# Long convolutions with the inverse second stage in float32r parts and a first stage that stacks both parts of two residues on its rows

## The chip, the core and the metric

The kernel runs on one core of a Trainium2 chip. The metric is the device time of one execution in microseconds. The engines are TensorE (PE in the profile; PEld are its weight loads), VectorE (DVE), ScalarE (ACT), GpSimd (POOL) and SyncE (SP), which here only starts transfers. Each engine works through its own instructions in order; semaphores make it wait for another engine or for a DMA.

## What is computed

One layer of a bidirectional encoder: a normalisation, one input projection, two head groups (four mLSTM heads and a Hyena operator of order two), an output projection and a squared-ReLU MLP. The change lies in the Hyena part, whose two long convolutions over 2048 positions and 512 channels are written in the reference as an FFT of length 4096:

```python
def two_sided_fft_conv(u, k_fwd, k_bwd, bias):
    kern = jnp.concatenate([k_fwd, jnp.zeros_like(k_fwd[:1]), k_bwd[:0:-1]], axis=0)
    K = jnp.fft.rfft(kern, axis=0)
    U = jnp.fft.rfft(u, n=2 * S, axis=1)
    y = jnp.fft.irfft(U * K[None], n=2 * S, axis=1)[:, :S]
    return y + u * bias
...
z = cv[..., OFF_HV:OFF_HV + H_WIDTH]
z = cv[..., OFF_HX1:OFF_HX1 + H_WIDTH] * two_sided_fft_conv(z, filt[:, 0, 0], filt[:, 1, 0], fb[0])
z = cv[..., OFF_HX2:OFF_HX2 + H_WIDTH] * two_sided_fft_conv(z, filt[:, 0, 1], filt[:, 1, 1], fb[1])
```

## The kernel before

The transform of 4096 points is done as two stages of 64 (4096 = 64 x 64), each a product with a constant matrix on TensorE over tiles of 128 rows by 512 channels. The first stage works on the positions that share a residue modulo 64: 16 tiles h in a convolution, four residues in each tile of input. Its result goes to DRAM (`d1`), sorted by the 32 frequencies j of the first stage. The second stage takes one j at a time, here called a turn: it transforms the kernel's tile (`dk`, made earlier by `filter_spectra`) and the data's tile (`d1`) with the same matrix `c_s2[j]`, multiplies the two spectra, and transforms back with `c_s2i[j]`; that result goes to DRAM (`d2`). Between the two convolutions the inverse first stage is done (`py`), the gate is multiplied in, and the first stage of convolution 1 follows at once (`first`, with o = 1). The inverse first stage of convolution 1 comes much later and is not touched.

Most products are float32 products made of three float32r ones. `split` writes a rounded upper part on one engine (`hi`, ACT) and the rest on another (`low`, POOL or DVE), and `mm3` adds up w_low x_hi, w_hi x_low and w_hi x_hi (lines 159 to 161). The inverse second stage is the exception: it multiplies whole float32 operands (line 1187), which the chip runs as two instructions.

In a turn of the second stage (lines 1175 to 1204, all from `hyena`) the names are: `prepare(j)` splits the matrix and the two tiles of residue j; `pk` is the kernel's spectrum (made by `spectrum`, copied to SBUF by `kept`); `pu` is the data's spectrum; `product(j)` multiplies them on DVE into `z`; `pi` is the inverse product for the turn before last, copied to `st` by ACT and stored. Loads are started three turns ahead (`kernel_loads`, `data_loads`), with the inverse matrix `ci` in its own turn. Tiles come from rings by tag: 6 tiles `raw`, 4 `hi`, 4 `z`, 4 `c`, 2 `cr`, 3 `ci`. A load into a ring waits until the tile's last reader is done, and SP holds all later loads behind it.

The order is that of the program text, for each engine alone. The long convolutions run as a generator, and each `yield` names how much of the input projection (`work`: matrix products, their evictions and stores) is put in before the generator goes on (`drive`). So the projection's products stand between those of the convolution on TensorE, and its casts, scalings and loads between the others on their engines.

Of the kernel before, what the change touches and what calls it, by code (L numbers as in the profile page):

```python
# [8 lines left out]
F32 = mybir.dt.float32  # L9
# [18 lines left out]
SPLIT = {"w4", "s1k"}  # L28
# [16 lines left out]
def host_constants():  # L45
# [15 lines left out]
    s1 = np.zeros((128, 2, 128))  # L61
    s1i = np.zeros((128, 2, 128))
# [4 lines left out]
    for b in range(4):  # L67
        q, r = slice(b, 128, 4), slice(b * 32, b * 32 + 32)
        s1[q, 0, q] = re
        s1[q, 1, q] = im  # L70
        s1i[r, 0, q] = wre.T / 4096
        s1i[r, 1, q] = wim.T / 4096
# [33 lines left out]
    data_row = (p % 2) * 64 + 4 * ((p % 32) // 2) + p // 32  # L106
# [8 lines left out]
    out["c_s1"] = pack(s1, "s1")  # L115
    out["c_s1i"] = pack(s1i, "s1i")
    out["c_s1k"] = pack(s1k, "s1k")
    out["c_s2"] = np.ascontiguousarray(s2[:, data_row, :], dtype=f32)
    out["c_s2i"] = np.ascontiguousarray(s2i[:, :, back_col], dtype=f32)
# [23 lines left out]
    out["c_t"] = np.ascontiguousarray(-np.stack([tn[64 * pa + 8 * (g // 4) + g % 4 + 4 * pb] for g in range(32)], axis=1))  # L143
# [4 lines left out]
class Builder:  # L148
# [258 lines left out]
    def filter_spectra(self, kp, wk, ps, ps2):  # L407
# [20 lines left out]
        def filt(i):  # L428
            g, o = divmod(i, 2)
            lg = lt[g % NB]  # L430
            if o == 0:
                for e in range(2):
                    rows = slice(64 * e, 64 * e + 64)
                    b = 8 * (g // 4) + g % 4
                    src = hv[rows, b:b + 5:4, :]
# [21 lines left out]
        def spread(i, x):  # L457
# [7 lines left out]
            if o == 1:  # L465
                self.load(self.dk.rearrange("j (b h q) o c -> b h j q o c", b=4, h=8)[g % 4][g // 4], st)
# [586 lines left out]
    def hyena(self, pools):  # L1053
# [6 lines left out]
        def raw(src):  # L1060
            t = wk.tile([128, 512], F32R, tag="raw", name="raw", bufs=6)
# [10 lines left out]
        def cols():  # L1072
            return wk.tile([128, 256], F32R, tag="c", name="c", bufs=4)

# [17 lines left out]
        def short(dtype=F32):  # L1092
            return wk.tile([128, 512], dtype, tag="z", name="z", bufs=4)

        def first(o, h, s1, x):

            st, dst = pair(), d1[o].rearrange("j (b h r) c -> h j b r c", b=4, h=16)[h]
            pts = []
            for r in range(2):
                pts.append(bank("p1"))  # L1100
                self.mm3(pts[r], s1[r], x, True, True)
# [3 lines left out]
            self.store(dst, st)  # L1105


        s1 = constant("c_s1")
        x = [raw(self.tile_rows(0, h)) for h in range(4)]
        self.load(self.s1i, io["c_s1i"])  # L1110
        yield 8.0
        s1, y = s1(), {0: parts(x[0])}
        yield 2.0
        for h in range(16):
            if h + 1 < 16:
                y[h + 1] = parts(x[h + 1])
            if h + 4 < 16:
                x.append(raw(self.tile_rows(0, h + 4)))
# [3 lines left out]
        for o in range(2):  # L1122
            kd, rd, c2, ci, kk, zz, pu = ({} for _ in range(7))

            def kernel_loads(j):
                c2[j] = wk.tile([128, 128], F32, tag="cr", name="cr", bufs=2)
                self.load(c2[j], io["c_s2"][j])
# [853 lines left out]
```

## Time and profile before

| | |
|---|---|
| median of 3 runs | 2696.65 us (2690.52 to 2699.77) |
| profiled execution | 2695.04 us |
| its span, first to last instruction | 2693.1 us |
| mean granted TensorE clock | 0.986 |
| PE busy | 2590.1 us, 96% of the span |
| DVE, ACT, POOL busy | 1544.1, 1232.0, 1204.1 us |
| moved by DMA | 465.74 MB, mean 173 GB/s |

Rows of the profile read "line engine operation out<-in shape xcount". Names are the program's with buffer numbers left out, and a line may be that of a helper: line 166 is ACT's cast in `split`, 169 its subtraction, 159 to 161 are the products of `mm3`, 231 and 234 start loads and stores. Rows of the timeline begin with the start in us from the first instruction and the duration in us; what stands in brackets at the end is the idle time before, and what ended it. PE's durations overlap from one product to the next.

The long convolutions lie between about 392 and 1013 us, beside the input projection. Convolution 0 has its first stage until about 465 and its turns from 482; the part between the convolutions runs from about 698 to 797, the turns of convolution 1 from 812.

### The profile page before, as it was taken

Reading aid. Unit: us, or ns where it says so; the run is one execution under the profiler, and the core shown is the slowest. Engines: PE = TensorE matmul, PEld = TensorE weight load, DVE = VectorE, ACT = ScalarE, POOL = GpSimd, SP = SyncE. Lnnn points to the kernel's source line nnn. Section 1 sums busy time; section 2 is a strip of 40 time slices with the busy share of each in tenths; the row PEclk is TensorE's granted clock in tenths of the full one; section 3 lists DMA queues with packets and bytes.
Section 4 is the critical chain, followed back from the end, with each engine's and each line's share of the span. In section 5 each row is a group of like instructions: output and inputs, shape, how many; then the busy total and the mean of one; then the engine's idle time right before and its main releaser. Section 6 shows DMA issues by size and latency. Waiting matters only on the chain.

```text
span 2693.1 us, 35367 instructions
## 1 busy us (share of the span) xinstructions
PE 2590.1 (96%) x12237; PEld 2110.8 (78%) x12237; DVE 1544.1 (57%) x2454; ACT 1232.0 (46%) x2276; POOL 1204.1 (45%) x964
## 2 busy tenths in 40 slices
PE   6999999999999998889997999999999999999998
PEld 5778888777798887767774788868888888888876
DVE  5676653777547665666556444474444443543477
ACT  6355544655544346653334444454444323222344
POOL 1211114555225543446666877677772440301232
PEclk8999999999999999999998999999999999999999
DMA  6233346665676558556765444554447453445555
GB/s 175 61 87 113 114 125 219 194 190 176 217 233 178 185 167 275 180 166 218 241 200 186 156 137 164 184 191 172 146 155 287 147 176 100 130 141 163 181 170 213
DMA packets 288355, 465.74 MB, mean 173 GB/s; under 512 B 37543, under 2 KB 149415, under 8 KB 287153
## 3 DMA queue, kind: packets, MB, share of 16 engines
q1 hardware_dynamic: 227600, 324.85, 38.8%
q10 hardware_dynamic: 53264, 117.53, 11.6%
q0 software_dynamic: 7312, 21.11, 3.1%
q8 instruction: 97, 1.59, 0.2%
q14 instruction: 82, 0.66, 0.1%
HBM read 289.27 MB, written 174.13 MB: 172 GB/s over the span
## 4 chain that ended last, share of the span: by engine, by line
PE 40%; DVE 4%; POOL 4%; DMA 3%; issue 2%; ACT 2%; ACTq 0%; SPq 0%; DVEq 0%; POOLq 0%
PE pm L159 13%; PE pm L160 13%; PE pm L161 13%; DVE cb L169 1%; POOL xt L1265 1%; DMA m<-in_w_mlp_out_dram 1%; DMA hm<-ht 1%; DMA m<-in_w_mlp_in_dram 1%; POOL cb L169 1%; ACT xo L1405 1%; DVE hm L1906 0%; ACTq L234 0%; DVE xo L1408 0%; DVE gss L1307 0%; DVE hm L169 0%
## 5 line engine op out<-in xcount | busy, mean ns | idle before, releaser
L166 ACT CAST cb<-m 128x1024 fp32r<-128x1024 f32 (+1 forms) x342 | 277.9, 849 | 438.0 <-PE pm L159 375.3
L169 DVE TENSOR_TENSOR cb<-m,cb 128x1024 fp32r<-128x1024 f32 (+1 forms) x222 | 237.8, 1109 | 301.0 <-ACT cb L166 300.7
L160 PE MATMUL pm<-cb 128*128 128x512 f32 x880 | 343.6, 390 | 7.8 <-DVE cb L169 7.8
L159 PE MATMUL pm<-hm,cb 128*128 128x512 f32 x840 | 330.8, 394 | 13.9 <-POOL cb L169 8.0
L159 PE MATMUL pm<-cb 128*128 128x512 f32 x880 | 342.4, 389 | 1.2 <-DVE cb L169 1.0
L161 PE MATMUL pm<-cb 128*128 128x512 f32 x880 | 342.6, 389 | 0.0
L160 PE MATMUL pm<-hm,cb 128*128 128x512 f32 x840 | 329.9, 393 | 2.6 <-POOL hm L169 2.5
L161 PE MATMUL pm<-hm,cb 128*128 128x512 f32 x840 | 328.9, 392 | 0.0
L169 POOL TENSOR_TENSOR cb<-m,cb 128x1024 fp32r<-128x1024 f32 x120 | 262.0, 2194 | 61.7 <-ACT cb L166 61.6
L1717 DVE TENSOR_TENSOR m<-pm,m 128x512 f32<-128x512 f32 x224 | 153.9, 690 | 235.0 <-PE pm L161 214.3
L159 PE MATMUL pt<-hn,w 128*128 128x512 f32 x640 | 267.7, 419 | 1.0 <-ACT hn L489 0.9
L169 POOL TENSOR_TENSOR raw<-raw,hi 128x512 fp32r<-128x512 f32 x160 | 206.4, 1302 | 103.0 <-ACT hi L166 76.7
L160 PE MATMUL pt<-hn,w 128*128 128x512 f32 x640 | 252.0, 394 | 0.3 <-DVE hn L490 0.2
L161 PE MATMUL pt<-hn,w 128*128 128x512 f32 x640 | 251.9, 394 | 0.0
L160 PEld LDWEIGHTS pm<-cb 128*128 128x128 f32 x880 | 165.2, 188 | 45.7 <-DVE cb L169 11.7
L159 PEld LDWEIGHTS pm<-hm,cb 128*128 128x128 f32 x840 | 159.0, 189 | 50.0 <-POOL cb L169 10.2
L159 PEld LDWEIGHTS pm<-cb 128*128 128x128 f32 x880 | 165.2, 188 | 36.4 <-ACT junk L1891 1.4
L161 PEld LDWEIGHTS pm<-cb 128*128 128x128 f32 x880 | 165.3, 188 | 33.8
L160 PEld LDWEIGHTS pm<-hm,cb 128*128 128x128 f32 x840 | 159.4, 190 | 36.6 <-POOL hm L169 2.9
L1721 ACT ACTIVATE m<-m 128x512 f32<-128x512 f32 x128 | 80.6, 630 | 233.9 <-DVE m L1717 232.3
L161 PEld LDWEIGHTS pm<-hm,cb 128*128 128x128 f32 x840 | 159.4, 190 | 33.6
L647 POOL DMA_DIRECT2D vp<-vst x96 | 61.3, 643 | 228.1 <-ACT vst L643 227.0
(323 smaller groups left out, 5732.5 us busy)
## 6 DMA issues: line engine op xcount, KB each, us to landing
ga<-m ACTq DMA_DIRECT2D x96, 512.0 KB, 3.4
m<-ga SPq DMA_DIRECT2D x96, 512.0 KB, 4.1
d<-st ACTq DMA_DIRECT2D x64, 512.0 KB, 2.6
m<-in_w_mlp_in_dram SPq DMA_DIRECT2D x64, 512.0 KB, 4.0
m<-in_w_mlp_out_dram SPq DMA_DIRECT2D x114, 256.0 KB, 3.6
raw<-d SPq DMA_DIRECT2D x96, 256.0 KB, 3.0
xt<-in_x_dram SPq DMA_DIRECT2D x32, 512.0 KB, 5.5
dk<-kst SPq DMA_DIRECT2D x32, 512.0 KB, 3.3
```

Source lines behind the costliest of these rows:

```text
L159: pe.matmul(ps, w[1], x[0], start=first, stop=False)
L160: pe.matmul(ps, w[0], x[1], start=False, stop=False)
L161: pe.matmul(ps, w[0], x[0], start=False, stop=last)
L166: self.act.copy(hi, src)
L169: (eng_lo or self.dve).tensor_tensor(lo, src, hi.bitcast(F32), ALU.subtract)
L647: pool.dma_start(dst[:, 8 * b + e:8 * b + 8:2, cc:cc + 128], st[64 * e:64 * e + 64])
L1265: eng.tensor_tensor(res[:, cs], tmp[e], res[:, cs], ALU.add)
L1405: act.activation(x1, xt, AF.Square, accum_out=ss1[:, h:h + 1])
L1717: dve.tensor_tensor(dst, a, b, ALU.add)
L1721: act.activation(g, g, AF.Relu)
```

## The change

Two things change in what is computed, and several in what carries it.

First, the inverse second stage uses `mm3`. Its matrix comes from the host in two parts (256 columns, upper part and rest), as does now `c_s2`; ACT rounds both with one copy (`rounded`), and the subtraction for `c_s2` on POOL is gone. The data `z` is split on the device: a cast on ACT and a subtraction on POOL, one turn after `product` made it.

Second, the first stage no longer takes 128 rows of upper parts and then 128 rows of rests. A tile has 64 positions of two residues; for each half of the tile, `stacked` makes one operand whose one half of the rows holds the upper part of a residue pair and whose other half holds its rest. One product with the upper part of the matrix on both halves, and one with the rest of the matrix on one half and zeros on the other, give what three products gave. The residues are grouped otherwise for this (two neighbouring ones, so `vp` is loaded straight and `d1` is stored in two pieces), and with them the rows of `c_s2` and the filter table. The split of z between the convolutions is made by DVE in halves.

Third, the rings: `raw` has 5 tiles instead of 6, `z` 5 instead of 4, `ci` is gone, and both matrices share the 2 tiles `cr`, now 256 columns wide. With these, `prepare(j + 1)` has moved behind the copy of spectrum j, the data is loaded two turns ahead and the matrix `c_s2` two turns ahead, after the kernel tile.

```diff
+        def stacked(src, tag, eng):
+            ts = [wk.tile([128, 512], F32R, tag=tag, name="hl", bufs=4 if tag == "hi" else 5) for _ in range(2)]
+            for t, p in zip(ts, (slice(0, 64), slice(64, 128))):
+                act.copy(t[p], src[p])
+            for t, p, q in zip(ts, (slice(0, 64), slice(64, 128)), (slice(64, 128), slice(0, 64))):
+                eng.tensor_tensor(t[q], src[p], t[p].bitcast(F32), ALU.subtract)
+            return ts
...
-            for r in range(2):
-                pts.append(bank("p1"))
-                self.mm3(pts[r], s1[r], x, True, True)
+            for g in range(2):
+                pts.append(bank("p1"))
+                pe.matmul(pts[g], s1[0], x[g], start=True, stop=False)
+                pe.matmul(pts[g], s1[1 + g], x[g], start=False, stop=True)
                 yield
...
             for j in range(34):
-                if j + 1 < 32:
-                    prepare(j + 1)
                 if j < 32:
                     pk = spectrum(j)
                     yield 1.3
                     kept(j, pk)
+                    if j + 1 < 32:
+                        prepare(j + 1)
+                    if j + 2 < 32:
+                        data_loads(j + 2)
...
-                    pe.matmul(pi, ci.pop(j - 2), zz.pop(j - 2), start=True, stop=True)
+                    self.mm3(pi, ci.pop(j - 2), zz.pop(j - 2), True, True)
...
+                if 1 <= j < 33:
+                    ci[j - 1] = rounded(ci[j - 1])
+                    zz[j - 1] = parts(zz[j - 1], short(F32R))
                 if j + 3 < 32:
                     kernel_loads(j + 3)
-                    data_loads(j + 3)
-                if j < 31 or j == 31:
-                    ci[j] = wk.tile([128, 128], F32, tag="ci", name="ci", bufs=3)
-                    self.load(ci[j], io["c_s2i"][j])
+                if j + 2 < 32:
+                    c2[j + 2] = matrix(io["c_s2"][j + 2])
+                if j < 32:
+                    ci[j] = matrix(io["c_s2i"][j])
```

How the instructions move on three engines, in a turn of convolution 0. What stands in brackets are the engines and queues that a row waits for. On TensorE (`pt` are the projection's products), before:

```order
L159 MATMUL pk_5014<-hi_4947,c_4944 128x512 [waits Activation_49,Pool_49]
L160 MATMUL pk_5014<-raw_4860,c_4944 128x512 [waits Pool_49]
L161 MATMUL pk_5014<-hi_4947,c_4944 128x512
...
L1187 MATMUL pi_5029<-z_4938,ci_4928 128x512 [waits DMAHW0_49,DVE_49,Activation_49]
L159 MATMUL pt_5031<-hn10_82,w1_92 128x512
```

and in the changed kernel:

```order
L163 MATMUL pk_5108<-hi_5059,c_5057 128x512 [waits Activation_49]
L164 MATMUL pk_5108<-raw_4949,c_5057 128x512 [waits Pool_49]
L165 MATMUL pk_5108<-hi_5059,c_5057 128x512
...
L163 MATMUL pi_5133<-hi_5080,c_5077 128x512 [waits Activation_49]
L164 MATMUL pi_5133<-z_5079,c_5077 128x512 [waits Pool_49]
L165 MATMUL pi_5133<-hi_5080,c_5077 128x512
```

The inverse product waited for DVE and for its matrix; it is now three products, of which the first waits for ACT and the second for POOL.

On SP's queue, where the loads of the second stage stand, before (`raw` from `dk` and `d10` are the kernel's and the data's tile, `qk0` is a store of the projection):

```order
L231 DMA cr_4548<-in_c_s2_dram 128x128 [waits DMAHW4_49,Pool_49]
L231 DMA raw_4550<-dk_65 128x512 [waits DMAHW5_49,PE_49]
L231 DMA raw_4552<-d10_3501 128x512 [waits DMAHW6_49,PE_49]
L231 DMA ci_4554<-in_c_s2i_dram 128x128 [waits DMAHW7_49,DMAHW0_49]
L231 DMA qk0_69<-yc_93 128x512 [waits DMAHW0_49,DVE_49]
```

and in the changed kernel:

```order
L235 DMA raw_4507<-d10_3501 128x512 [waits DMAHW5_49,PE_49]
L235 DMA raw_4541<-dk_65 128x512 [waits PE_49,Pool_49]
L235 DMA cr_4543<-in_c_s2_dram 128x256 [waits DMAHW3_49,Activation_49]
L235 DMA cr_4545<-in_c_s2i_dram 128x256 [waits DMAHW4_49,DMAHW1_49,Activation_49]
L235 DMA qk0_69<-yc_93 128x512 [waits DMAHW2_49,DVE_49]
```

The matrix `c_s2` stood ahead of the two tiles of its residue and now stands behind the kernel tile of the residue after it; both matrices now wait for ACT.

On ACT, before, from one copy of a spectrum (`z<-pk`) on:

```order
L1147 COPY z_5026<-pk_5014 128x512 [waits PE_49]
L607 ACTIVATE yc_93<-pt_4957,cw_64 128x512 [waits DMAHW1_49,PE_49]
L1193 COPY st_5028<-pi_5029 128x512 [waits DMAHW2_49,PE_49]
L166 CAST c_5065<-cr_4978 128x128 [waits DMAHW2_49]
L166 CAST hi_5068<-raw_4980 128x512 [waits DMAHW3_49,Pool_49]
L166 CAST hi_5071<-raw_4982 128x512 [waits DMAHW4_49,PE_49,Pool_49]
```

and in the changed kernel:

```order
L1173 COPY z_4842<-pk_4830 128x512 [waits PE_49]
L1086 CAST c_4844<-cr_4820 128x256 [waits DMAHW7_49]
L170 CAST hi_4846<-raw_4740 128x512 [waits DMAHW6_49]
L170 CAST hi_4849<-raw_4789 128x512 [waits DMAHW4_49,Pool_49]
L610 ACTIVATE yc_93<-pt_4764,cw_64 128x512 [waits DMAHW1_49,PE_49]
L1222 COPY st_4854<-pi_4855 128x512 [waits DMAHW3_49,PE_49]
L1086 CAST c_4875<-cr_4822 128x256 [waits DMAHW0_49]
L170 CAST hi_4878<-z_4824 128x512 [waits DVE_49,Pool_49]
```

The three casts of `prepare` stood behind the copy of `pi` and now stand ahead of it, behind the copy of the spectrum; the rounding of the inverse matrix and the cast of z are new behind it.

## What I predict, and from what

> **What bounds the kernel now.** I read the page first (TensorE is busy for 96% of the span), then cut the busy times at the borders of the long convolutions, then asked what TensorE itself waits for there. Columns of the first view: stretch, its length, busy time and instructions of PE, PEld, DVE, ACT and POOL, granted clock, DMA share, GB/s.
>
> ```profile
> 392.00:469.00 77.00, 77.00 (x355) 62.91 (x355) 28.78 (x53) 31.36 (x56) 36.46 (x39) 1.00 0.66 221
> 469.00:690.00 221.00, 221.00 (x911) 170.50 (x910) 164.35 (x271) 122.68 (x231) 113.20 (x113) 1.00 0.62 188
> 690.00:800.00 110.00, 107.46 (x619) 94.10 (x618) 56.92 (x110) 52.25 (x96) 31.68 (x26) 0.98 0.70 228
> 800.00:1013.00 213.00, 210.00 (x1400) 185.03 (x1398) 140.84 (x245) 98.92 (x197) 106.53 (x110) 0.99 0.58 176
> ```
>
> These are the first stage of convolution 0, its 32 turns, the part between the convolutions, and the 32 turns of convolution 1. TensorE is idle for 5.5 of 621 us. The waits of TensorE in the same time (engine line <- releaser: sum, times, longest) are as few:
>
> ```profile
> PE pt L159 <- ACT w L166: 2.1, 1, 2.1
> PE py L159 <- ACT hi L166: 1.3, 1, 1.3
> PE py L160 <- POOL raw L169: 0.8, 1, 0.8
> ```
>
> So this stretch lasts as long as its products, and those of the projection are poured in between by fixed weights that the change leaves alone. A product removed here is worth its full time, and any new wait of TensorE costs its full time: the rest of the program follows behind.
>
> **What the change removes.** The timeline of TensorE around one inverse product (start, duration, engine, operation):
>
> ```profile
> 565.55 0.40 PE L161 MATMUL pt<-hn,w 128*128 128x512 f32 x1
> 565.78 1.02 PE L1187 MATMUL pi<-z,ci 128*128 128x512 f32 x2
> 566.24 0.80 PE L159 MATMUL pt<-hn,w 128*128 128x512 f32 x1
> 566.88 0.40 PE L160 MATMUL pt<-hn,w 128*128 128x512 f32 x1
> ```
>
> Durations overlap, so the price is the distance of starts: 0.23 us from one float32r product to the next. From 565.55 to 566.88 are 1.33 us; less two plain products (0.46) the float32 inverse takes 0.87 us. Three parts take 0.69. That saves 0.18 us, 64 times (the copies of `pi` below count them): 11.5 us.
>
> ```profile
> L159 PE MATMUL p<-hi,c x64: 389/397/497, 401.6 to 795.8; 128*128 128x512 f32 x64
> L1193 ACT COPY st<-pi x64: 574/586/594, 492.4 to 1013.5; 128x512 f32<-128x512 f32 x64
> ```
>
> The first stage has 64 groups of three products; each becomes two: 64 x 0.23 = 14.7 us. **Together 26 us less TensorE work**, all in stretches where it is never free.
>
> **What it adds beside TensorE.** Durations of the operations (last columns: busy us, mean ns; the second row is a copy of one partition row):
>
> ```profile
> L166 ACT CAST hi<-raw 128x512 fp32r<-128x512 f32 x160 | 95.6, 619 | 37.3 <-POOL c L169 11.4 <-PE pu L161 8.7 <-DMA raw<-d 4.8
> L1151 ACT COPY st<-pk 1x512 f32<-1x512 f32 x2 | 1.2, 578 | 0.0
> L166 ACT CAST c<-cr 128x128 fp32r<-128x128 f32 x64 | 18.9, 296 | 13.5 <-ACT st L1193 6.0 <-DMA raw<-dk 2.6 <-DVE vst L729 2.6
> L166 ACT CAST c<-z 128x256 fp32r<-128x256 f32 x2 | 0.7, 402 | 0.0
> L169 POOL TENSOR_TENSOR raw<-raw,hi 128x512 fp32r<-128x512 f32 x144 | 185.7, 1303 | 76.2 <-ACT hi L166 62.2 <-PE py L159 9.0 <-PE pk L161 1.6
> L169 POOL TENSOR_TENSOR c<-cr,c 128x128 fp32r<-128x128 f32 x64 | 31.2, 487 | 171.9 <-ACT c L166 156.0 <-PE pi L1187 8.9 <-PE pu L161 7.0
> ```
>
> A turn gains on ACT the cast of z (0.62), the rounding of the inverse matrix (0.40) and 0.11 for the wider c_s2: 1.13 us, 36 in 32 turns. POOL gains a subtraction (1.30) and loses the one on the matrix (0.49): 26 us. ACT then works 159 of about 215 us, POOL 139: neither is full. In convolution 0's first stage ACT has a second cast for each of 16 tiles (one row costs 0.58 us where 128 cost about the same, so 64 rows are no cheaper) and POOL a second subtraction. No row shows 64 rows on POOL; between half and the whole price it gains 0 or 20.8 us, and I take the whole, as ACT goes. That is 57 of some 70 us, near full, but the second half is only wanted one product group later, so I charge nothing; if this cover fails, up to 5 us. Each half is stored by itself: 32 more issues on ACT's queue, under its idle time. The filter table and the straight loads of `vp` change addresses, not counts: nothing.
>
> Between the convolutions DVE makes the lower parts of z in two halves. The nearest place in the trace:
>
> ```profile
> 736.45 1.30 POOL L169 TENSOR_TENSOR raw<-raw,hi 128x512 fp32r<-128x512 f32 x1 [5.85 <-ACT hi L166]
> ...
> 737.20 1.10 DVE L169 TENSOR_TENSOR z<-z,hi 128x512 fp32r<-128x512 f32 x1 [0.26 <-ACT hi L166]
> ...
> 743.55 0.69 DVE L169 TENSOR_TENSOR raw<-raw,hi 128x512 fp32r<-128x512 f32 x1
> ...
> 746.65 0.39 PE L160 MATMUL py<-raw,c 128*128 128x512 f32 x1
> ```
>
> The operand that DVE finishes at 744.24 is used at 746.65: 2.4 us of cover. One more cast (0.62, 0.52 of it before the next can start) and one more subtraction (0.69) eat 1.2. Nothing is charged. The subtraction at 737.20 took 1.10 instead of 0.69 while POOL ran until 737.75: if each of the 16 new ones were held for a whole POOL operation, 1.30 us, the cover would be short by 0.1 us a tile, 2 us in all. The Trainium skill, "SBUF — State Buffer", section "Who interferes with whom", says that a DVE instruction with two SBUF inputs and a GpSimd instruction that reads SBUF exclude each other, the later one waiting for the whole of the earlier; the 1.10 us agree. By that rule the change puts exactly such instructions on both engines, and the sum would lose those 2 us.
>
> **What it makes late.** The order shows the second-stage matrix loaded one turn later than before, behind the load of the next kernel tile, which waits for `pu`'s products. One turn of before:
>
> ```profile
> 569.16 0.39 PE L161 MATMUL pu<-hi,c 128*128 128x512 f32 x1
> 569.36 0.32 SPq L231 DMA_DIRECT2D raw<-d  x1
> ...
> 569.73 0.42 SPq L231 DMA_DIRECT2D ci<-in_c_s2i_dram  x1
> ...
> 577.37 0.39 PE L160 MATMUL pk<-raw,c 128*128 128x512 f32 x1
> ...
> 557.12 0.39 PE L161 MATMUL pu<-hi,c 128*128 128x512 f32 x1
> ...
> 563.26 0.39 PE L160 MATMUL pk<-raw,c 128*128 128x512 f32 x1
> ...
> DMA to landing us min/median/max: 2.8/4.5/6.2
> DMA to landing us min/median/max: 2.4/2.6/4.9
> raw<-dk SPq DMA_DIRECT2D x64, 256.0 KB, 3.6
> ```
>
> The landing rows are those of `cr`, `ci` (64 KB each) and `raw<-dk`. In the changed kernel the load that waits for `pu` issues at 569.36, the matrix (now 128 KB) 0.37 later, and lands between 2.4 and 6.2 us after. I take 3.6, the tile it stands next to in the queue. Then follow on ACT the rounding (0.40) and the cast of the kernel tile (0.62), on POOL 1.30, and some 0.1 of hand-over: 0.37 + 3.6 + 2.4 = 6.4 us. The product that needs it is the `pk` after next, second part, 8.0 us later, 7.6 once two turns are 0.18 shorter. So most turns keep 1.2 us of slack that was a whole turn before. In the short ones (557.3 to 563.26: 5.9, then 5.5) 0.9 is missing; reading the turns I find about three in each convolution: 5 us.
>
> The starts and ends have no full turn to hide in:
>
> ```profile
> 482.83 0.39 PE L161 MATMUL pk<-hi,c 128*128 128x512 f32 x1
> ...
> 485.37 0.39 PE L160 MATMUL pk<-raw,c 128*128 128x512 f32 x1
> ...
> 676.85 0.69 DVE L1165 TENSOR_TENSOR z<-z,pu 128x512 f32<-128x512 f32 x1
> ...
> 677.99 1.02 PE L1187 MATMUL pi<-z,ci 128*128 128x512 f32 x2
> ...
> 1011.56 0.69 DVE L1165 TENSOR_TENSOR z<-z,pu 128x512 f32<-128x512 f32 x1
> 1012.35 1.10 PE L1187 MATMUL pi<-z,ci 128*128 128x512 f32 x2
> ```
>
> At the start, `prepare` of turn 1 now follows the copy of turn 0's spectrum: from 483.2 two copies (1.1, the Nyquist row is one), 0.40, 0.62 and 1.30 lead to 486.7, where TensorE wanted the operand at 485.4: 1.3, twice, 2.6 us. At the end the last z is ready at 677.54 and 1012.25 and went straight into the product; now a cast and a subtraction (2.1 with hand-over) stand between, less the 0.2 by which the second part is later: 1.4 and 1.8, 3.2 us. In the turns the same cast and subtraction have over one turn and cost nothing, except where `pi` follows `pk` at once; 1 us for those. Given back: 5 + 2.6 + 3.2 + 1 = 12 us.
>
> **The sum.** The profiled execution took 2695.04 us (span 2693.1 and 1.9 around it), 1.6 under the median of 2696.65, inside the spread of 9. 2695.0 - 26 + 12 = 2681 us; I say **2681**, its own range 2674 to 2688.
>
> **The rivals.** (a) *No new wait counts*: matrices land in 2.6 us like `ci` did, the edges hide under projection products. 2695 - 26 = 2669. For it: TensorE hardly waited before; against it: the last z of convolution 1 demonstrably had nothing to hide under. 0.25.
> (b) *The matrix load sets the turn.* If it takes 5.3 us, between the median and the maximum of `cr`, the chain is 8.1 us against 7.6, and with ACT then late for the copies of `pi` too I put 0.6 a turn: 64 x 0.6 = 38, 2695 - 26 + 38 = 2707, slower. It decides from 26/64 = 0.41 us lost a turn, a landing of about 5.1. For it: `cr`'s own median of 4.5, and 8 MB more traffic; against it: `ci` at 2.6 and `raw<-dk` at 3.6. 0.10.
> (c) *The queues fill up*: ACT and POOL take things in order, and POOL near full in the first stage (5) plus late lower parts of z behind scaled weights in a third of the turns (21 x 0.5 = 10) come on top of the 12: 2696, no change. 0.16.
> (d) *DVE held by POOL* in each of the 16 tiles, as worked out above: 2 us more, 2683. For it: the 1.10 us; against it: POOL has one such operation a tile there. 0.04. The forecast keeps 0.45.
>
> **How the numbers follow.** A measurement of this kernel can tell about 0.3%, 8 us, from no change: 2688.6 to 2704.7. Faster: nearly all of the forecast (0.42), (a) and (d): 0.71. Same: 0.03 of the forecast and most of (c), some of (b): 0.20. Slower: 0.09. The range reaches from (a) with the runs' spread, 2666, to (c), 2697; outside it stay (b) and the edges of (a) and (c).
>
> **What would show it.** TensorE's busy time in the four stretches falls by about 26 us and its waits grow from 5 to some 17. A wait of `pk` on POOL's `raw` at the start of each convolution and in short turns confirms the late matrix; ACT waiting for DMA `cr` in nearly every turn is its sign. The last `pi` should wait on POOL's z for 1 to 2 us. If ACT waits for `cr` over 2 us a turn, (b) is at work; if TensorE shows no waits at all, (a). I am wrong altogether if three float32r parts start more than 0.29 us apart, since then the inverse saves nothing.

## The result and the profile after

The changed kernel takes 2736.18 us, median of 4 runs (2735.98 to 2736.85), beside 2698.21 (2690.52 to 2699.93) for the kernel before on the same chip: **slower, ratio 1.0154, 95% interval 1.0141 to 1.0166**. Forecast were 2681 us and a range of 2666 to 2697. The profiled execution has a span of 2734.1 us, 41.0 longer, at a granted clock of 0.980 (0.986).

The same four stretches as in the prediction, with their borders moved to where the same work now lies (columns: stretch, its length, busy time and instructions of PE, PEld, DVE, ACT and POOL, granted clock, DMA share, GB/s):

```profile
392.00:479.00 87.00, 78.33 (x330) 61.14 (x330) 28.71 (x53) 43.56 (x73) 55.95 (x54) 0.92 0.64 203
479.00:715.00 236.00, 222.98 (x946) 175.24 (x945) 164.04 (x271) 149.62 (x295) 138.56 (x113) 1.00 0.62 194
715.00:827.00 112.00, 103.32 (x583) 89.56 (x582) 69.78 (x126) 63.08 (x113) 31.03 (x25) 0.95 0.69 226
827.00:1053.00 226.00, 213.28 (x1437) 193.91 (x1436) 149.62 (x245) 127.23 (x262) 132.97 (x109) 0.98 0.61 189
```

They last 661 us instead of 621, though about 26 us of products are gone. TensorE, which had been busy almost all the time, is now idle in every one of them and has a lower granted clock in three. ACT and POOL are still far from full: 44 and 56 of 87 us in the first stage. What TensorE waited for between 392 and 1053 us (engine line <- releaser: sum, times, longest):

```profile
PE pi L164 <- POOL z L173: 10.7, 14, 1.8
PE pk L164 <- POOL raw L173: 7.2, 10, 1.1
PE p L1129 <- ACT st L1132: 4.5, 2, 3.0
PE py L163 <- ACT hi L170: 4.3, 4, 1.8
PE p L1129 <- POOL hl L1115: 4.1, 5, 2.7
PE pi L163 <- ACT hi L170: 3.4, 5, 1.0
PE py L164 <- DVE raw L173: 3.1, 5, 1.0
PE pk L163 <- ACT hi L170: 2.1, 4, 1.3
```

All such waits together are 42.4 us in 54 places; before they were 5.4. In the order of the program: 8.6 in the first stage, 12.8 in the turns of convolution 0, 8.7 between, 12.3 in the turns of convolution 1. No single wait stands out, and every operand that is split on the device is among them.

The starts of the `pk` products give the same by stage and can be compared from kernel to kernel, so the table below uses them: first `pk`, the 32 turns of convolution 0 from first to last `pk`, from there to the first `pk` of convolution 1, and its turns.

| profiled execution of | turns begin at | turns 0 | between | turns 1 |
|---|---|---|---|---|
| before | 482.4 | 187.0 | 143.2 | 190.7 |
| after | 492.5 | 199.5 | 147.9 | 201.1 |
| before, less the products that the change removes | 475 | 181 | 136 | 185 |

The last line takes 32 x 0.23 us off the first stage and off the part between, and 32 x 0.18 off each convolution's turns. Against it the changed kernel loses 17, 18, 12 and 16 us, and some 3 behind the last turn: about 67 us, of which 26 are the products saved and 41 the longer span.

**A loop of queues in the first stage.** ACT (with ACTq, the DMA issues that stand in its queue), POOL and TensorE around 445 us in the changed kernel, put in order of time for each engine (start, duration, engine, operation, in brackets the idle time before and what ended it):

```profile
440.69 1.26 ACT L1113 CAST hl<-raw 64x512 fp32r<-64x512 f32 x2 [1.57 <-DVE yc L616]
445.19 0.62 ACT L170 CAST w<-wf 128x512 fp32r<-128x512 f32 x1 [3.24 <-POOL wf L550]
445.72 0.58 ACT L1132 COPY st<-p 128x512 f32<-128x512 f32 x1
446.33 1.37 ACTq L238 DMA_DIRECT2D d<-st  x2
447.74 1.26 ACT L1113 CAST hl<-raw 64x512 fp32r<-64x512 f32 x2 [1.44 <-DVE st L1133]
...
441.39 2.65 POOL L1115 TENSOR_TENSOR hl<-raw,hl 64x512 fp32r<-64x512 f32 x2 [0.86 <-ACT hl L1113]
444.12 1.04 POOL L550 TENSOR_TENSOR wf<-wf,eps 128x512 f32<-128x512 f32 x1
448.49 2.61 POOL L1115 TENSOR_TENSOR hl<-raw,hl 64x512 fp32r<-64x512 f32 x2 [3.33 <-ACT hl L1113]
...
446.44 0.47 PE L1129 MATMUL p<-hl,c 128*128 128x512 f32 x1 [1.58 <-ACT st L1132]
449.80 0.80 PE L1129 MATMUL p<-hl,c 128*128 128x512 f32 x1 [2.65 <-POOL hl L1115]
450.39 0.63 PE L1130 MATMUL p<-hl,c 128*128 128x512 f32 x1
450.82 0.63 PE L163 MATMUL pt<-hn,w 128*128 128x512 f32 x1
```

Read it as a circle. POOL's two subtractions (2.65) wait for ACT's two casts; the scaling of a weight tile of the projection (`wf`, 1.04) stands behind them on POOL; ACT's cast of that weight waits 3.24 us for it; behind it on ACT stand the copy of `p`, which TensorE waits for, the issue of two stores (1.37 us from first to last), and the next tile's casts; for these POOL is idle 3.33 us, and TensorE 2.65. By their busy time POOL is idle for a third of the stage and ACT for half of it, and each is late for the other. The two stores are new in kind as well: before, a tile had one, and its issue took 0.33 us of ACT's queue:

```profile
447.09 0.33 ACTq L234 DMA_DIRECT2D d<-st  x1
```

**The same scaling in a turn, and the late matrix.** Four rows around 587 us, then SP, ACT, POOL and TensorE around 575:

```profile
585.94 0.62 ACT L170 CAST w<-wf 128x512 fp32r<-128x512 f32 x1 [3.13 <-POOL wf L550]
587.25 0.62 ACT L170 CAST hi<-z 128x512 fp32r<-128x512 f32 x1
588.01 1.28 POOL L173 TENSOR_TENSOR z<-z,hi 128x512 fp32r<-128x512 f32 x1 [2.10 <-ACT hi L170]
589.34 0.51 PE L164 MATMUL pi<-z,c 128*128 128x512 f32 x1 [0.92 <-POOL z L173]
...
572.78 0.62 SPq L235 DMA_DIRECT2D cr<-in_c_s_dram  x1
576.53 0.41 ACT L1086 CAST c<-cr 128x256 fp32r<-128x256 f32 x1 [2.60 <-DMA cr<-in_c_s_dram]
577.54 2.53 POOL L173 TENSOR_TENSOR raw<-raw,hi 128x512 fp32r<-128x512 f32 x2 [2.71 <-ACT hi L170]
578.88 0.49 PE L164 MATMUL pk<-raw,c 128*128 128x512 f32 x1 [0.61 <-POOL raw L173]
```

In the first, ACT stands 3.13 us at a weight of the projection's next column block, which TensorE does not need yet, and the lower part of z, whose cast stands behind it, comes 0.92 us late for `pi`. In the second the matrix issued at 572.78 is awaited by ACT for 2.60 us and `pk` is 0.61 late. ACT's own waits over 380 to 1060 us, first after, then before:

```profile
ACT w L170 <- POOL wf L550: 59.1, 21, 5.2
ACT c L1086 <- DMA cr<-in_c_s_dram: 44.5, 31, 5.9
...
ACT w L166 <- POOL wf L547: 35.7, 15, 4.6
```

**A pause costs more than its length.** After the pause that ends at 449.80 the products start 0.43 us apart (450.39 to 450.82) where they started 0.23 apart in the prediction's rows. Another pause of the changed kernel's first stage:

```profile
415.73 0.76 PE L1129 MATMUL p<-hl,c 128*128 128x512 f32 x1 [2.96 <-ACT st L1132]
...
420.13 0.63 PE L163 MATMUL pt<-hn,w 128*128 128x512 f32 x1
420.56 0.60 PE L164 MATMUL pt<-hn,w 128*128 128x512 f32 x1
420.99 0.40 PE L165 MATMUL pt<-hn,w 128*128 128x512 f32 x1
```

From 415.73 to 420.99 TensorE starts 12 products in 5.26 us; at 0.23 they take 2.76. The pause of 2.96 us cost 2.5 more. The Trainium skill, "TensorE: Matmul & The Clock Gate", Part 1, says that the array falls to half its clock after an idle window of about 3.4 us and returns after a busy one; the spacing of 0.43 against 0.23 agrees, but here a pause shorter than that was enough. Short waits, too, cost more than is listed: `pi` starts at 587.92 and 589.34, 1.42 apart instead of 0.23, with 0.92 listed, so 0.27 more. As an estimate from this one wait, 54 waits at 0.27 make some 15 us.

### The profile page after: what moved, and what is told of

It reads as the page before. It is cut to its first block, busy times and chain, and to the rows that moved or that the text cites. A ratio compares the mean times of both kernels' runs of the same rounds, so it can differ in the third digit from the quotient of the medians.

```text
span 2734.1 us, 35354 instructions
## 1 busy us (share of the span) xinstructions
PE 2591.6 (95%) x12237; PEld 2117.7 (77%) x12237; DVE 1556.0 (57%) x2470; ACT 1309.6 (48%) x2438; POOL 1274.3 (47%) x978
## 3 DMA queue, kind: packets, MB, share of 16 engines
q10 hardware_dynamic: 57872, 117.53, 11.5%
## 4 chain that ended last, share of the span: by engine, by line
PE 39%; DVE 5%; POOL 3%; DMA 2%; issue 2%; ACT 2%; ACTq 0%; SPq 0%; DVEq 0%; POOLq 0%
PE pm L163 13%; PE pm L164 13%; PE pm L165 13%; DVE cb L173 1%; DVE hm L173 1%; POOL xt L1299 1%; DVE m L1751 1%; DVE hm L1940 1%; ACT xo L1439 0%; PE pm L161 0%; DVE hm L1870 0%; POOL cb L173 0%; DMA hm<-ht 0%; DMA m<-in_w_mlp_out_dram 0%; DMA m<-in_w_mlp_in_dram 0%
## 5 line engine op out<-in xcount | busy, mean ns | idle before, releaser
L173 POOL TENSOR_TENSOR raw<-raw,hi 128x512 fp32r<-128x512 f32 x144 | 185.8, 1309 | 220.5 <-ACT hi L170 193.7
L163 PEld LDWEIGHTS pm<-cb 128*128 128x128 f32 x880 | 165.1, 188 | 35.7 <-ACT junk L1925 1.4
```

Of the source, the lines that this page charges most:

```text
L163: pe.matmul(ps, w[1], x[0], start=first, stop=False)
L173: (eng_lo or self.dve).tensor_tensor(lo, src, hi.bitcast(F32), ALU.subtract)
```

## The experiments

Times are medians; the ratio is to the kernel before, run on the same chip (2694 to 2698 us); turns and waits are those of each run's profiled execution. Two explanations were on the table from the start: that the matrices come late, and that ACT and POOL, which take their work in order, are held up by the new splits. A letter in an expectation is that batch's own name for one of them.

**One part undone.** `inv_f32` is the changed kernel with one float32 product for the inverse, as before, and the `ci` tiles that go with it:

```diff
-                    self.mm3(pi, ci.pop(j - 2), zz.pop(j - 2), True, True)
+                    pe.matmul(pi, ci.pop(j - 2), zz.pop(j - 2), start=True, stop=True)
...
-                    ci[j - 1] = rounded(ci[j - 1])
-                    zz[j - 1] = parts(zz[j - 1], short(F32R))
```

> The changed kernel (2736 us) with the inverse second stage back in one float32 product: no cast, no subtraction of z, the inverse matrix in its own ring of 3; the matrix c_s2 is still loaded behind the kernel tile and prepare still stands behind the copy of the spectrum; z has 4 tiles. The float32 products cost 64 x 0.18 = 12 us more. Theory A (the late matrix c_s2 makes the new waits in the turns): those 35 us stay, 2743 to 2748 us. Theory B (ACT and POOL, each in order, now wait for each other too long, because POOL has one more subtraction in a turn and ACT two more casts): most of the 35 us go, 2718 to 2726 us.

2721.63 us (1.010, 1.0082 to 1.0118). The part that should save 11.5 us costs 14.5: without it the turns of convolution 0 take 189.7, those of convolution 1 still 201.9.

`first_old` has the first stage of the kernel before in both convolutions (three products from `parts`, one store a tile):

```diff
-                pe.matmul(pts[g], s1[0], x[g], start=True, stop=False)
-                pe.matmul(pts[g], s1[1 + g], x[g], start=False, stop=True)
+                self.mm3(pts[r], s1[r], x, True, True)
...
-            for g in range(2):
-                self.store(dst[g], st[:, g])
+            self.store(dst, st)
```

> The changed kernel with the first stage of before in both convolutions (three products, one cast, one subtraction, one store a tile, and the residues grouped as before); the turns as in the changed kernel. It gives up 64 x 0.23 = 15 us. If the stacked operands are what costs 17 us in the first stage and 12 us between the convolutions: 2736 + 15 - 24 to 29 = 2722 to 2727 us, and TensorE has almost no idle time in those two stretches. If what costs there is something else (the rings, the order): 2745 to 2751 us.

2725.17 (1.0114, 1.0095 to 1.0132). Here too the part that saves 14.7 us of products costs 11: turns begin at 485.0, and 144.4 us lie between the convolutions.

`order_only` undoes both: the arithmetic of before in the order and the rings of after.

> The changed kernel's order of the convolution turn (preparation behind the spectrum product, matrix load behind the stores, split inverse stage), its ring sizes, but the first stage of the kernel before and one float32 product for the inverse second stage. No term of product time is saved. Theory B2 (the rearranged turn is itself a loss, from the late matrix and from operands asked for later): the two earlier runs are nearly additive, so about 2721.6 + 2725.2 - 2736.2 = 2710.6; 2704 to 2717, and the second convolution's turns stay near 200 us. Theory A (the loss comes only from the new splits, the order is harmless): 2691 to 2699, second convolution's turns near 191 us.

2706.5 (1.005, 1.0034 to 1.0067): 12 us are lost by the arrangement alone. Turns take 192.1 and 199.8 us. ACT waits for the matrix as in the changed kernel:

```profile
ACT c L1082 <- DMA cr<-in_c_s_dram: 59.5, 38, 7.3
```

`moved6` asks which part of the arrangement it is. It is the kernel before, all six `raw` tiles kept, with nothing but the lines moved:

```diff
-                if j + 1 < 32:
-                    prepare(j + 1)
                 if j < 32:
...
                     kept(j, pk)
+                    if j + 1 < 32:
+                        prepare(j + 1)
+                    if j + 2 < 32:
+                        data_loads(j + 2)
...
                     kernel_loads(j + 3)
-                    data_loads(j + 3)
+                if j + 2 < 32:
+                    matrix_load(j + 2)
```

> The kernel before, with nothing but the places of three things moved as the change moves them (preparation behind the spectrum product, data load in the middle of the turn, matrix load at its end), its ring of six raw tiles and all its products kept. The run with before's arithmetic in the changed order and rings took 2706.5, 12 above the kernel before. If the places cost it: 2703 to 2710, with the second convolution's turns near 200 us. If the ring of five raw tiles (or the wider matrix load) costs it: 2692 to 2698, turns near 191 us.

2698.89 over 10 runs, 1.0014 (1.0005 to 1.0024). The moved lines cost some 4 us. The matrix is no longer late, even in the profiled execution, which was the longest of the ten:

```profile
ACT c L166 <- DMA cr<-in_c_s_dram: 5.7, 3, 3.6
```

So most of the 12 us comes with what `order_only` has beside the moved lines, above all five `raw` tiles and a matrix twice as wide. The two were not tried apart, but both show in the traces: between 830 and 1010 us SP's loads wait 96 us for products of `pu` and `pk`, which free the tiles, in `order_only` and 76 in `moved6`, and the median time from the matrix's issue to its landing is 3.7 us against 2.7.

**The late matrix alone.** `c2_early` loads the matrix of the second stage ahead of the data tile:

```diff
                     if j + 2 < 32:
+                        c2[j + 2] = matrix(io["c_s2"][j + 2])
                         data_loads(j + 2)
...
-                if j + 2 < 32:
-                    c2[j + 2] = matrix(io["c_s2"][j + 2])
```

> The changed kernel with the load of the matrix c_s2 started half a turn earlier, ahead of the load of the data tile instead of behind the kernel tile; nothing else. Theory A: ACT's waits for the matrix (44 us in the changed kernel) fall under 10 and the turns give back 20 to 30 us: 2706 to 2716 us. Theory B: only the second convolution's turns gain, where no weight scaling stands in POOL's queue: 2724 to 2732 us.

2725.21 (1.0112, 1.0091 to 1.0134). ACT's waits for `cr` fall from 44.5 to 5.8 us and each convolution's turns by 5 us (194.1, 195.8). A real cause, and over a quarter of the 38 to 41 us. Theory A expected two to three times as much; the time falls in theory B's range, but not by its mechanism, since both convolutions gain.

**More time for the operands.** `prep_first` is `c2_early` with `prepare(j + 1)` back ahead of the spectrum product; `ahead2` makes the stacked operands of the first stage two tiles ahead:

```diff
+        y[1] = stacked(x[1].bitcast(F32), "z", pool)
         for h in range(16):
-            if h + 1 < 16:
-                y[h + 1] = stacked(x[h + 1].bitcast(F32), "hi", pool)
+            if h + 2 < 16:
+                y[h + 2] = stacked(x[h + 2].bitcast(F32), "z" if h % 2 else "hi", pool)
```

> Matrix loads ahead of the data loads, as in the earlier run of that edit (2725.2), and the preparation of the next turn ahead of the spectrum product as in the kernel before. If the place of the preparation is part of the loss: turns of 188 to 191 us in the first and 188 to 193 in the second convolution, 2708 to 2718. If it is not: 194 and 196, 2722 to 2728. A rival on the other side: preparation ahead of the kept product delays the split of the inverse operand, which then comes later than the product wants it; then 2730 to 2740.

> The first stage of the first convolution has its stacked operands made two tiles ahead in place of one. If the stall there is latency of one chain (raw tile, cast, subtraction, then the product), the first group of the turns starts at 475 to 485 us in place of 492.5 and the time is 2722 to 2729. If it is throughput (POOL's subtractions and the weight scaling share one queue and ScalarE's cast waits behind them), the start stays at 490 to 495 and the time at 2734 to 2739.

2726.59 (1.0125, 1.011 to 1.014) and 2735.6 (1.0151, 1.0135 to 1.0167). Neither gains on its counterpart (`c2_early` and the changed kernel). In `ahead2` turns begin at 492.9: a lead of one tile more is worth nothing where the queues, not the distance, set the pace.

**Work moved to another engine.** `scale_dve` scales the weights on DVE during the convolutions, `z_dve` makes the lower part of z there, `c2z` adds `c2_early` to it, `stack_mix` deals the two subtractions of a stacked pair to POOL and DVE, `best1` does all four:

```diff
-            self.pool.tensor_tensor(raw, raw, nw.unsqueeze(2).to_broadcast([128, nk, n]), ALU.mult)
+            (self.dve if self.conv else self.pool).tensor_tensor(raw, raw, nw.unsqueeze(2).to_broadcast([128, nk, n]), ALU.mult)
...
-                    zz[j - 1] = parts(zz[j - 1], short(F32R))
+                    zz[j - 1] = parts(zz[j - 1], short(F32R), dve)
...
-        s1, y = s1(), {0: stacked(x[0].bitcast(F32), "hi", pool)}
+        s1, y = s1(), {0: stacked(x[0].bitcast(F32), "hi", (pool, dve))}
```

> The changed kernel with the scaling of the projection's weights on DVE instead of POOL from the start of the long convolutions on, so that ACT's cast of a weight no longer waits for POOL (59 us in 21 waits in the changed kernel). Theory B: the first stage gives back some 8 and the turns of convolution 0 some 12 us: 2714 to 2720 us. Theory A: no change, 2733 to 2739 us.

> The changed kernel with the lower part of the spectrum product z subtracted on DVE instead of POOL in the turns; nothing else. If POOL is the engine that delivers the lower parts too late in the turns of convolution 0 (TensorE's waits for POOL's z: 10.7 us, and for POOL's raw: 7.2 us in the changed kernel), these waits fall under 6 us together, the 32 turns of convolution 0 go from 199.5 to 188 to 194 us, and the whole to 2722 to 2730 us. If ACT's late cast of z is the cause instead, the wait only changes its name: 2733 to 2739 us.

> Both in one: the matrix c_s2 loaded ahead of the data tile, and the lower part of z on DVE. If the two causes of the turns are independent, the gains of the two single kernels add up: with 10 us for the first and 6 to 14 for the second 2712 to 2720 us. If they are the same lateness, the pair gives no more than the better one: 2722 to 2726 us.

> The changed kernel with the two half-height subtractions of each stacked operand on two engines: POOL and DVE in the first stage, DVE and POOL between the convolutions. If one engine's doubled subtraction is what makes the stacked operands late: the first convolution's turns begin 6 to 8 us earlier, the stretch between the convolutions is 3 to 6 us shorter, 2722 to 2728 us. If it is ACT (two casts, two stores for one): no change, 2733 to 2739 us.

> All four edits: the early matrix, the lower part of z on DVE, the two halves of the stacked operands on two engines, and the scaling of the projection's weights on DVE during the long convolutions. By the sum of the single causes (10, 6 to 14, 9 to 13, 4) 2695 to 2707 us, about the time before; if the saving of 26 us on TensorE comes through as well, 2670 to 2690 us. DVE then works some 90% of the time in the turns of convolution 0; if that makes it the late engine, 2710 us or more.

2731.56 (1.0141, 1.0122 to 1.016), 2729.8 (1.0133, 1.0114 to 1.0152), 2730.65 (1.0135, 1.0119 to 1.0151), 2741.92 (1.0171, 1.0154 to 1.0189) and 2763.76 (1.0256, 1.0241 to 1.0271). What one stage gains another loses: with the scaling on DVE the turns begin at 484.7, 8 us sooner, but convolution 0's take 201.6; with z on DVE they take 192.7, but convolution 1's 205.1. DVE has its own in-order work there. Of the first four only `z_dve` lies in a range that was expected, at its edge; `scale_dve` fell between its two, and `c2z` and `stack_mix` missed both of theirs. `best1` fell in its last range, far from the sum of its gains: four edits, three of which gain alone, lose 28 us together.

`best3` combined `prep_first` and `ahead2` with z's lower part on DVE in convolution 0 only and both gate operands on POOL:

> prep_first, with stacked operands two tiles ahead, the lower part of the inverse operand on VectorE in the first convolution (POOL in the second), and both lower parts of the gate operands on POOL. If the gains add: 2695 to 2708; to beat the kernel before it must come under 2694. If ScalarE and POOL share one limit whatever the order, each gain hands its wait to the next operand and the time is 2715 to 2730.

2724.95 (1.0112, 1.0097 to 1.0128). No sum of gains: convolution 0's turns take 186.8 us, but they begin at 493.9, so the first stage keeps its loss, and 150.6 us lie between the convolutions.

**The circle opened.** Three edits leave every operation with its engine and move only when or from which queue something is issued: `c2_early` above, and two more. `store_sp` has SP issue the stores of the first stage, so that they leave ACT's queue:

```diff
             for g in range(2):
-                self.store(dst[g], st[:, g])
+                self.load(dst[g], st[:, g])
```

> The stores of the first stage are issued by SP and no longer by ScalarE. Theory Q (a loop of queues: ScalarE waits for POOL's scaled weights, POOL's scaling stands behind the two subtractions, these wait for casts that stand on ScalarE behind the stores): each store pair holds ScalarE for 1.2 to 1.5 us of a loop of about 7.5 us, so of some 17 us lost in the first stage 5 to 10 come back; turns begin at 483 to 488, time 2726 to 2731. Theory R (the stall is the subtractions' own time on POOL, whoever issues the stores): turns begin at 491 to 494, time 2734 to 2738. On the other side: SP now waits for the stores' data ahead of its loads, tiles come late, 2740 or more.

2722.33 (1.0105, 1.0088 to 1.0122), better than expected: turns begin at 483.6, and 142.1 us lie between the convolutions instead of 147.9.

`scale_early` issues the scaling of a weight tile on POOL one step of the projection before ACT casts it, instead of right before:

```diff
-            else:
-                weights.setdefault(c, []).append(chunk(fetched[c][step - 1]))
+                return
+            if step > 1:
+                weights.setdefault(c, []).append(chunk(fetched[c][step - 2], True))
+            if step < 3:
+                scale(fetched[c][step - 1])
...
-            if live and b == 1:
-                ahead(i // 4 + 1, 0)
+            if live and b < 2:
+                ahead(i // 4 + 1, b)
```

The last lines start the load of a weight tile earlier too, by one block of the projection.

> The weights of the projection are scaled on POOL one step (about a third of a block's products, then a whole block) before ScalarE casts them, so that ScalarE has them when it comes to the cast. No operation is added. Theory Q: ScalarE's 59 us of waits for scaled weights in the stretch fall below 15, the loop of queues is open; the first stage gains 8 to 14, the turns 3 to 8 together: 2715 to 2726. Theory R (the engines are short of time, not of order): the waits move to another releaser and the time stays at 2730 to 2738. On the other side: the scaling comes ahead of a lower part that TensorE wants sooner: above 2740.

2718.52 (1.0083, 1.0068 to 1.0098): 17.7 us come back with not one operation less. Turns begin at 481.6, those of convolution 0 take 194.1. ACT's wait for scaled weights, 59.1 before the edit:

```profile
ACT w L170 <- POOL wf L550: 11.6, 4, 4.2
```

The earlier load makes room for the earlier scaling, but late loads were not what ACT waited for: between 380 and 1060 us POOL waits for such a load twice in both kernels, 14.1 us in the changed one and 14.0 here.

`before_se` is the control: the same edit on the kernel before.

> The kernel before with nothing but the scaling of weights one step earlier. If the loop of queues is something that only the change closes, TensorE has nothing to gain here and the time stays within 0.3% of the kernel before: 2687 to 2703. If the gain of that edit (18 us on the changed kernel) is there whatever the kernel, 2676 to 2684, and it says nothing on the change.

2693.08 over 11 runs, ratio 0.9997 (0.9988 to 1.0005): nothing, though the same wait of ACT fell there too, from 35.7 to

```profile
ACT w L166 <- POOL wf L547: 11.9, 4, 4.6
```

So the edit undoes a loss that the change made. Before, ACT waited at the same place, and TensorE had cover for it. The other two edits have no such control: `store_sp` was not tried on the kernel before, where a tile has one store, and there the matrix is loaded early already.

`se_c2_st` joins `scale_early`, `c2_early` and `store_sp`:

> Scaling early, stores of the first stage by SP, and the matrix load ahead of the data load (2725.2 by itself) together. If the three are separate causes: -11 from the matrix, -10 to -20 from the other two: 2705 to 2716. To beat the kernel before, under 2694, it would have to return all but 15 of the 64 us. If they share a cause: 2715 to 2725.

**2691.4 us over 10 runs, ratio 0.9988 (0.9979 to 0.9997)**. This is 14 us better than the best that was expected. The three gains, 17.7 + 11.0 + 13.9 = 42.6, add up (44.8), so none of them only handed its wait on to the next operand. In the first stage alone, where `scale_early` and `store_sp` work on the same circle, they bring the turns forward by 10.9 and 8.9 us apart and by 16.2 together, nearly all of the 17 that were lost. It is the only version of the changed kernel that comes out below the kernel before, by about 3 us, at the edge of what can be told. Its stretches, cut at the prediction's borders but for the first, and TensorE's waits in them (16.7 us in all):

```profile
392.00:473.00 81.00, 80.59 (x372) 65.61 (x371) 34.09 (x60) 48.47 (x81) 59.98 (x57) 1.00 0.75 236
473.00:690.00 217.00, 214.53 (x930) 173.74 (x929) 167.73 (x268) 148.84 (x296) 140.73 (x112) 1.00 0.65 206
690.00:800.00 110.00, 105.85 (x655) 94.14 (x654) 69.50 (x133) 63.68 (x113) 29.80 (x24) 0.98 0.71 237
800.00:1013.00 213.00, 202.77 (x1370) 184.59 (x1369) 144.97 (x234) 123.32 (x255) 130.78 (x108) 0.98 0.64 195
...
PE pi L164 <- POOL z L173: 4.0, 8, 0.9
PE pk L164 <- POOL raw L173: 3.7, 6, 0.9
```

In the first stage POOL is now *busier* (60 of 81 us) and ACT too (48), and TensorE has hardly a pause; its granted clock there is 1.00 again. Turns begin at 476.3 and take 183.9 in convolution 0, close to the products alone (475 and 181); between the convolutions it is 140.2 (136), in convolution 1 196.4 (185). What is left is mostly in that last one.

`best4` tried that: `se_c2_st`, but both matrices loaded from ACT's queue, behind the cast that frees their tile.

```diff
                 c2[j] = rounded(c2[j])
+                if 1 <= j < 31:
+                    c2[j + 1] = matrix(io["c_s2"][j + 1], self.store)
...
+                    ci[j] = matrix(io["c_s2i"][j], self.store)
```

> Scaling early and stores of the first stage by SP as in the run that took 2691.4, but both matrices of a turn are now loaded by ScalarE's own queue, right behind the cast that frees their tile, in place of SP behind other loads. If the late matrices are the cause of what the second convolution still loses there (196 us of turns against 185 from its products; a wait of 2.1 us behind a matrix is followed by 6 us of slow products): 188 to 192 us of turns, 2682 to 2688. If the 64 issues more on ScalarE take as much as they give: 2689 to 2695. On the other side: ScalarE's casts come later than the products want them, 2697 to 2705.

2699.97 over 11 runs, 1.0022 (1.0013 to 1.0031), a miss of the kind foreseen on the other side: turns of 189.8 and 200.0 us. ACT's casts now stand behind its own issues, 77 times:

```profile
ACT hi L170 <- ACT c L1090: 33.2, 77, 0.8
```

## Why the prediction was wrong

**The saving was right.** The parts of an inverse product start 0.23 us apart, as priced; first and last of one in the changed kernel, two steps apart:

```profile
575.11 0.39 PE L163 MATMUL pi<-hi,c 128*128 128x512 f32 x1
...
575.56 0.39 PE L165 MATMUL pi<-hi,c 128*128 128x512 f32 x1
```

Where TensorE is well fed, it shows: in `se_c2_st` the turns of convolution 0 take 183.9 us against 187.0 before, and they begin 6 us sooner.

**What failed is the cover.** The sum gave back 12 us of 26. The runs lost 67: 17 in the first stage and 12 between the convolutions, where the sum had nothing, and 18, 16 and 3 in the turns and behind them, where it had 12. Three sentences of the prediction carry the error. "ACT then works 159 of about 215 us, POOL 139: neither is full" was true (150 and 139 of 236 us in convolution 0) and no reason: two in-order queues that wait for each other were late here at half to two thirds of full load. The words "the second half is only wanted one product group later, so I charge nothing" look at one operand and not at what is queued behind it, the weight scaling on POOL, and behind that on ACT. "32 more issues on ACT's queue, under its idle time" took issues for free. The profile doesn't count them as busy, but a tile's two stores hold ACT's queue for 1.2 us and more in the first stage, where the one store before took 0.33. `scale_early` and `store_sp` price the scaling and the stores at 17.7 and 13.9 us over all stages; the forecast had 0, and 5 if the cover failed in the first stage.

**The split of z in the turns** was priced at 1 us beside the ends. `pi` waits 14.1 us for its parts; the two ends are 3.2 of that. `inv_f32` shows the whole, with the rings that go with it: the split inverse costs 14.5 instead of saving 11.5.

**The late matrix** was the right mechanism, sized too low: 5 us for short turns and 2.6 at the starts; `pk` waits 9.3 us for its operands, and `c2_early` gives 11 back. The chain was worked out as 6.0 us from the matrix's issue to the operand (6.4 less 0.37); in the rows around 575 us it runs from 572.78 to 578.81, half of POOL's 2.53 after 577.54. So the chain had its right length, and what was mis-sized is how often it is late: about six short turns were forecast, and ACT waits for the matrix in 31 of 64. Rival (b), a matrix that sets the turn, did not happen: its sign was over 2 us of ACT's waiting a turn, and it is 44.5 us in 64 turns. That the matrix is late so often comes from the five tiles or its width more than from the moved line, to which the prediction put it down.

**The ends** came out as forecast, 1.4 and 1.8 us, the first of them partly by luck: in convolution 0 the last `pi` waits only 0.53 us and the one before it 0.91; in convolution 1 the two parts of the last one wait 0.90 and 0.85.

**Between the convolutions** nothing was charged, at most 2 us for DVE held by POOL, rival (d). `py` waits 8.7 us, 4.3 of it for ACT's casts and 3.1 for DVE. Rival (d) wanted each of 16 new subtractions held for 1.30 us; in the trace DVE's 16 pairs of halves take 1.40 us a pair where nothing holds them, and 2.7 us more in all. `store_sp` shortens the stretch by 5.8 us, so the store issues on ACT were about half of the 12 lost here; what made the rest is open.

**A wait was charged at its length.** The forecast gives back 12 us of waits; listed are 37 more than before (42.4 less 5.4), and the loss is 67. The other 30 went into slower products. The forecast's sign, 26 us less busy time of TensorE in the four stretches, did not come: it rose from 615.5 to 617.9 us, so the products that are left take 28 us more. Some 15 of these are the 0.27 us around each wait, and some 13, an estimate from the granted clocks of the stretches (0.92, 1.00, 0.95 and 0.98, where they were 1.00, 1.00, 0.98 and 0.99), the products at 0.43 us after the long pauses.

Rival (c), "the queues fill up", named what happened and where; at 2696 us it had 15 us beyond the forecast's 12 for what took 55, because it added single late operands and not a circle.

Still open: what the last 22 us of `se_c2_st` are made of (2691.4 against 2695 less 26), beyond its 16.7 us of waits; five tiles against the wider matrix; and the rest of the part between the convolutions.

## What to carry to other kernels

Where an engine is bound and others feed it, don't stop at how busy these are; write down the order of each in-order queue around one added operation and follow who stands behind it, across engines, until the path ends or comes back to its start. A wait that costs nothing today (ACT at the scaled weights) is where the next added operation will hurt; issue such work one step early first. Count DMA issues as time of the queue that they stand in, and charge a pause of TensorE more than its length.

## What was not expected of the hardware

- Pauses of 2.65 us (two products after one of 1.58) and of 2.96 us were followed by products 0.43 us apart, for 5 us in the second case. In `se_c2_st` 2.08 us and a second wait of 0.71 were enough, after a stretch of steady work. Its next products of 256 columns start 0.21 us apart, where such products started 0.12 apart just before the pause:

```profile
858.03 0.28 PE L164 MATMUL pt<-w,hn 128*128 128x256 f32 x1
858.15 0.28 PE L165 MATMUL pt<-w,hn 128*128 128x256 f32 x1
860.51 0.64 PE L163 MATMUL pi<-hi,c 128*128 128x512 f32 x1 [2.08 <-ACT hi L170]
861.86 0.80 PE L164 MATMUL pi<-z,c 128*128 128x512 f32 x1 [0.71 <-POOL z L173]
...
863.09 0.42 PE L164 MATMUL pt<-w,hn 128*128 128x256 f32 x1
863.30 0.42 PE L165 MATMUL pt<-w,hn 128*128 128x256 f32 x1
```

- Left between half and the whole price in the prediction: a subtraction of 64 rows takes POOL as long as one of 128: 2.65 us for two of 64x512, 1.30 for one of 128x512. ACT's cast is alike, 1.26 for two halves, 0.62 for a whole tile. So stacking both parts on the rows doubled the price of the split here.
